# A hybrid decoder layer on one Trainium2 core: the samples' columns join the chunks' columns in the state space products, and the recurrence is spread over more steps

## The chip, the cores and the metric

The kernel runs on one core of a Trainium2 chip. The metric is the device time of one execution in microseconds. An execution uses five engines with queues of their own: TensorE (PE, matrix products, with its weight loads as PEld), VectorE (DVE), ScalarE (ACT), GpSimd (POOL) and SyncE (SP), which issues nearly all transfers. Each engine works through its queue in the order in which the program was written, and waits for others by semaphores.

## The reference

One layer of a hybrid decoder serves one prompt of 2048 tokens and 8 samples of 4 tokens with the same weights, all in fp32. Cut to the part that matters here:

```python
h = rms_norm(x, norm_mix); z = h @ w_in          # [u (512) | xin, B, C (3 x 512)]
y_ssm = s5_ssm(u, ...)                           # 32 groups of 16 channels, one 64-dim complex diagonal state each
#   s[t] = a * s[t-1] + Bbar @ u[t];  y[t] = Re(C @ s[t]) + D * u[t];  samples start from a given state s0
y_ssm = gelu(y_ssm); y_ssm = y_ssm * sigmoid(y_ssm @ w_glu + b_glu)
y_conv = B * causal_dwconv(C * xin, conv_w)      # width 3 over positions
x = x + concat(rms_norm(y_ssm), rms_norm(y_conv)) @ w_out
x = x + cross_attention(...)                     # 4 heads, 256 memory tokens
x = x + (gelu(causal_dwconv(h @ w_up)) * (h @ w_gate)) @ w_down
```

The results are the outputs of prompt and samples, the memory's keys and values, and the new states.

## The kernel before

Columns are positions: the 2048 + 32 tokens lie in five pieces of 416 columns, channels on the partitions. Every weight product is split in three products of rounded fp32 (`mm3`: hi x hi, hi x lo, lo x hi). `W` loads raw weight tiles (`wraw`), rounds them on ScalarE (`whi`) and takes the rest on GpSimd (`wlo`, two halves of 512 columns). `A` does the same for activations: `araw` is scaled and rounded on ScalarE (`xh`), the rest (`xl`) is taken on VectorE for even and on GpSimd for odd tiles. It has ten slots, eight for the piece in work.

The change lies in the second stage, the projections of the short-conv group. It runs over 10 pieces (two halves of five), each with two projections (`ct_`) of three outputs over eight tiles `k`: 20 projections of 72 products, 1440 in all. After each `k`, that is after nine products, a hook runs: in the second projection of a piece it frees the activation tile just used, then weights and activations are pumped, and then the streams `slow` and (every second hook) `slow2` go one step on. I call the nine products a group. After each projection come its convolution products: `xi`, `E` on VectorE, a scaled copy on ScalarE, two taps and a product on VectorE, and the last product `y` on GpSimd, whose store goes out with the next hook.

The state space work is written as generators in the stream `slow`, so a `yield` in them fixes how many groups lie between two of their parts:

- `state_inputs` first runs `phases` up to its mark (the tables of the recurrence, some 70 small VectorE instructions), copies the samples' inputs `us`, and then makes 16 input steps. Step `c` multiplies two input matrices `gc` with the chunk columns `uc` (256 columns, eight tokens each) and, in a second product, with the samples' columns (8), into one PSUM tile; ScalarE copies both into `st`. `turn` (complex turn by `ph`, on VectorE, every third on GpSimd) and `scan_blocks` (a scan of 16 blocks, its factors copied to `dz` by ScalarE) follow one and two steps later.
- `scan` closes the recurrence over the blocks.
- `toeplitz` (in `slow2`) prepares matrices; `state_outputs` waits for it and makes 16 output steps. In step `c`, `enter(c+1)` writes the entry states `scat` and the last state `sfin` (VectorE and GpSimd), `back(c+2)` turns the states back: a product `mc`, a sum, a product `mb` on VectorE, then `st` times `ph` on GpSimd. One group later TensorE multiplies `uc` and `scat` for two channel groups, and with two more products `us` and the samples' entry states `s0s`. ScalarE's GELU reads the PSUM tile, and the results are stored.

All four or eight products of a step stand in one place of TensorE's queue, and the PSUM tiles of these steps (`aux`) have two buffers. `uc`, `gc`/`tcn`, `scat` and `yg` have two buffers each as well. The loads of step `c+2` are written behind the products of step `c`.

Of the kernel before, what the change touches and what calls it, by code (L numbers as in the profile page):

```python
# [11 lines left out]
F32 = mybir.dt.float32  # L12
# [3 lines left out]
ALU = mybir.AluOpType  # L16
# [14 lines left out]
NCH = 256  # L31
# [6 lines left out]
PAUSE, STALL = "pause", "stall"  # L38
# [170 lines left out]
def tile_hymba_step(ctx: ExitStack, tc: tile.TileContext, I: dict, O: list):  # L209
# [25 lines left out]
    u_d = dt("u_d", [512, NB, NCH])  # L235
# [625 lines left out]
    def load_u(c):  # L861

        uc = py.tile([128, 2, NCH], F32, tag="uc", name="uc", bufs=2)
        for i in range(2):
            g = 2 * c + i
            SY.dma_start(out=uc[:, i, :], in_=u_d[16 * g:16 * g + 16].rearrange("p s c -> s p c"))
        return uc
# [65 lines left out]
    def blocks(c):  # L933
        return st[:, :, c, 8:264].rearrange("p r (k j) -> p r k j", j=16)

# [8 lines left out]
    def scan_blocks(c):  # L944

        S.copy(out=dz[:, :, 1:16], in_=rp[:, c, 0:1].unsqueeze(1).to_broadcast([128, 16, 15]))
        for r in range(2):
            x = st[:, r, c, 8:264]
            V.tensor_tensor_scan(out=x, data0=dz.rearrange("p k j -> p (k j)"), data1=x, initial=0.0, op0=ALU.mult, op1=ALU.add)

    def state_inputs():
# [15 lines left out]
        load(1)  # L967
        for step in tb:
            if step == "tables":
                break  # L970
            yield step
        V.tensor_copy(out=us_[64:128, 0], in_=us_[0:64, 1])
        for _ in range(4):
            yield PAUSE
        for c in range(16):
            uc, gc = ld.pop(c)
            for i in range(2):
                ps = aux()
                PE.matmul(ps[:, 8:264], lhsT=gc[:, i, :], rhs=uc[:, i, :], start=True, stop=True)
                PE.matmul(ps[:, 0:8], lhsT=gc[:, i, :], rhs=us_[:, 0, 2 * c + i, :], start=True, stop=True)  # L980
                h = slice(i * 64, (i + 1) * 64)
                S.copy(out=st[h, 0, c, :], in_=ps[0:64, 0:264])
                S.copy(out=st[h, 1, c, :], in_=ps[64:128, 0:264])
            if c + 2 < 16:
                load(c + 2)
            if c > 0:
                turn(c - 1, G if c % 3 == 1 else V)
            if c > 1:
                scan_blocks(c - 2)
            yield PAUSE  # L990
            next(tb, None)
            if c % 4 == 3:
                yield PAUSE
        turn(15, V)
        scan_blocks(14)
        rs_ = []
        for nm in ("state_ssm_re", "state_ssm_im"):
            r = py.tile([128, 128], F32, tag="sr", name="sr", bufs=2)
            SY.dma_start(out=r, in_=I[nm][0].rearrange("b (g a) n -> (b g) (a n)", a=2))
            rs_.append(r)  # L1000
        yield PAUSE
        scan_blocks(15)
        for _ in tb:
            yield PAUSE
        for _ in range(6):
            yield PAUSE
# [33 lines left out]
    def state_outputs():  # L1040
# [24 lines left out]
        def enter(c):  # L1065

            sc = py.tile([128, 2, 256], F32, tag="scat", name="scat", bufs=2)
            V.memset(sc[:, :, 0:1], 0.0)
            m1, m2 = parts.pop(c)
            for a in range(2):  # L1070
                h = slice(a * 64, (a + 1) * 64)
                for r in range(2):
                    (G if r else V).tensor_tensor(out=sc[r * 64:(r + 1) * 64, a, 1:256], in0=m1[h, r, 0:255],
                                                  in1=m2[h, r, 0:255], op=ALU.add if r else ALU.subtract)
            for r in range(2):
                G.tensor_tensor(out=sfin[:, r, c:c + 1], in0=m1[:, r, 255:256], in1=m2[:, r, 255:256],
                                op=ALU.add if r else ALU.subtract)
            ent_[c] = sc
# [15 lines left out]
        for c in range(16):  # L1094
            if c + 1 < 16:
                enter(c + 1)
            if c + 2 < 16:
                back(c + 2)
            yield PAUSE
            uc, tcn, oc = ld.pop(c)  # L1100
# [12 lines left out]
            G.tensor_copy(out=ysm[:, g2, :], in_=yg[:, :, 256:264])  # L1113
            for i in range(2):
# [17 lines left out]
    def scan():  # L1132
# [3 lines left out]
        cmul(sp_, sf[:, 0], sf[:, 1], s0[:, 0], s0[:, 1], a4[:, 0:1, :].to_broadcast(sh), a4[:, 1:2, :].to_broadcast(sh), sh, "scm")  # L1136
        V.tensor_tensor(out=sf, in0=sf, in1=st[:, :, :, 0:8].rearrange("p r g b -> p r b g"), op=ALU.add)
        yield PAUSE
# [5 lines left out]

        last = st[:, :, :, 8:264].rearrange("p r g (k j) -> p r g k j", j=16)[:, :, :, :, 15]
        m2, e = product_tile("b"), product_tile("b")
# [977 lines left out]
```

## Time and profile before

| what | before |
|---|---|
| median of three runs | 3051.72 us (3048.32 to 3055.66) |
| the profiled execution | 3054.09 us |
| its span, first to last instruction | 3052.0 us |
| mean granted clock | 0.98 |
| TensorE, products / weight loads busy | 2904.3 / 2804.3 us (95% / 92%) |
| VectorE, ScalarE, GpSimd busy | 1474.1 / 1109.6 / 1166.6 us |

The times in the rows further down count from the start of the span. A row of the timeline gives start, length, engine, line, operation, the tile written and the tiles read, the shape, and in brackets the idle time of the engine before it and who ended it. Products overlap: one of 128x416 lasts 0.35 us in the records, and the next starts 0.19 us after it. An fp32 product that is not rounded shows as two passes (x2). Behind the wait of a row the name tells who came last.

### The profile page before, as it was taken

The numbers are of one execution on the slowest core, as the hardware profiler recorded it, in microseconds if no ns is written. First come the engines' busy times: TensorE is split into PE (matmuls) and PEld (weight loads), VectorE is DVE, ScalarE is ACT, GpSimd is POOL, SyncE is SP. The second block draws the span as 40 slices with busy tenths as digits, with TensorE's granted clock in tenths as the row PEclk, the third lists the DMA queues.
The fourth block names the chain that finished last, engine by engine and source line by source line (L and its number), as shares of the span: only waits on it lengthen the run. The fifth ranks groups of instructions, "written<-read, shape, count | busy, mean of one in ns | idle before, by whom it ended". The sixth has DMA issues, their size and how long they took to land.

```text
span 3052.0 us, 42118 instructions
## 1 busy us (share of the span) xinstructions
PE 2904.3 (95%) x15728; PEld 2804.3 (92%) x15728; DVE 1474.1 (48%) x2698; ACT 1109.6 (36%) x2152; POOL 1166.6 (38%) x1304
## 2 busy tenths in 40 slices
PE   7868989989999999999999999999999999999998
PEld 6767989879999998999999999998999999989997
DVE  5769675364444344354643333436433433364444
ACT  5334322354445444343422222224222222243333
POOL 3663484354332003343523323233232232245653
PEclk9888989999999999999999999999999999999999
DMA  8553454365343123665532112124312122134331
GB/s 223 149 155 108 135 165 120 88 177 155 113 151 94 51 61 97 203 215 180 181 119 63 56 55 63 56 62 140 99 56 63 49 63 63 56 119 126 112 110 53
DMA packets 387340, 335.95 MB, mean 110 GB/s; under 512 B 81121, under 2 KB 361239, under 8 KB 387103
## 3 DMA queue, kind: packets, MB, share of 16 engines
q1 hardware_dynamic: 364079, 299.30, 33.1%
q10 hardware_dynamic: 23056, 33.96, 3.1%
q8 instruction: 124, 2.03, 0.3%
q14 instruction: 81, 0.66, 0.1%
HBM read 259.98 MB, written 75.29 MB: 110 GB/s over the span
## 4 chain that ended last, share of the span: by engine, by line
PE 57%; DVE 3%; DMA 1%; issue 1%; POOL 1%; ACT 1%; SPq 0%; ACTq 0%; DVEq 0%; POOLq 0%
PE g L368 5%; PE g L369 5%; PE g L367 5%; PE u L368 5%; PE u L367 5%; PE u L369 5%; PE d L367 5%; PE d L369 5%; PE d L368 5%; PE mm L368 3%; PE mm L369 3%; PE mm L367 3%; PE aux L368 1%; DVE t L1173 1%; POOL wlo L98 0%
## 5 line engine op out<-in xcount | busy, mean ns | idle before, releaser
L98 POOL TENSOR_TENSOR wlo<-wraw,whi 128x512 fp32r<-128x512 f32 x489 | 644.0, 1340 | 896.8 <-ACT whi L94 839.0
L367 PE MATMUL mm<-xh,whi 128*128 128x416 f32 x1600 | 584.2, 365 | 5.0 <-ACT whi L94 3.4
L368 PE MATMUL mm<-xl,whi 128*128 128x416 f32 x1600 | 571.9, 357 | 4.5 <-POOL xl L159 4.5
L369 PE MATMUL mm<-xh,wlo 128*128 128x416 f32 x1600 | 568.0, 355 | 3.0 <-POOL wlo L98 2.9
L2013 DVE TENSOR_TENSOR xac<-d,xac 128x416 f32<-128x416 f32 x440 | 258.5, 591 | 252.4 <-PE d L369 249.3
L94 ACT CAST whi<-wraw 128x1024 fp32r<-128x1024 f32 x256 | 267.0, 1046 | 172.5 <-PE d L368 129.5
L367 PE MATMUL d<-acth,whi 128*128 128x416 f32 x880 | 311.4, 354 | 19.1 <-DVE xac L2013 18.1
L367 PEld LDWEIGHTS mm<-xh,whi 128*128 128x128 f32 x1600 | 308.2, 193 | 12.8 <-ACT whi L94 4.0
L369 PEld LDWEIGHTS mm<-xh,wlo 128*128 128x128 f32 x1600 | 307.5, 192 | 8.2 <-POOL wlo L98 5.7
L368 PEld LDWEIGHTS mm<-xl,whi 128*128 128x128 f32 x1600 | 307.8, 192 | 7.6 <-POOL xl L159 5.9
L368 PE MATMUL u<-xl,whi 128*128 128x416 f32 x880 | 311.8, 354 | 1.4 <-POOL xl L159 0.7
L368 PE MATMUL g<-xl,whi 128*128 128x416 f32 x880 | 311.8, 354 | 0.0
L367 PE MATMUL u<-xh,whi 128*128 128x416 f32 x880 | 309.8, 352 | 1.2 <-ACT xh L158 1.1
L367 PE MATMUL g<-xh,whi 128*128 128x416 f32 x880 | 310.6, 353 | 0.0
L369 PE MATMUL d<-acth,wlo 128*128 128x416 f32 x880 | 309.6, 352 | 0.0
L369 PE MATMUL g<-xh,wlo 128*128 128x416 f32 x880 | 309.6, 352 | 0.0
L369 PE MATMUL u<-xh,wlo 128*128 128x416 f32 x880 | 308.5, 351 | 0.0
L368 PE MATMUL d<-actl,whi 128*128 128x416 f32 x880 | 307.9, 350 | 0.2 <-DVE actl L1994 0.2
L1173 DVE SCALAR_TENSOR_TENSOR t<-E,par,t 128x416 f32<-128x416 f32 (+1 forms) x220 | 154.5, 702 | 265.5 <-ACT t L1981 262.6
L159 POOL TENSOR_TENSOR xl<-araw,xh 128x416 fp32r<-128x416 f32 x100 | 114.6, 1148 | 385.5 <-ACT xh L158 357.6
L367 PEld LDWEIGHTS d<-acth,whi 128*128 128x128 f32 x880 | 165.2, 188 | 28.6 <-DVE xac L2013 25.9
L1990 DVE TENSOR_TENSOR t<-t,g 128x416 f32<-128x416 f32 x110 | 64.6, 587 | 260.3 <-PE g L369 260.1
(466 smaller groups left out, 4999.4 us busy)
## 6 DMA issues: line engine op xcount, KB each, us to landing
wraw<-in_w_up_dram SPq DMA_DIRECT2D x66, 512.0 KB
wraw<-in_w_gate_dram SPq DMA_DIRECT2D x66, 512.0 KB
wraw<-in_w_down_dram SPq DMA_DIRECT2D x66, 512.0 KB
araw<-x SPq DMA_DIRECT2D x120, 208.0 KB
xres<-x SPq DMA_DIRECT2D x80, 208.0 KB
x<-xo ACTq DMA_DIRECT2D x80, 208.0 KB
x<-xT ACTq DMA_DIRECT2D x40, 208.0 KB
araw<-oo SPq DMA_DIRECT2D x40, 208.0 KB
```

What stands on the lines that cost most here:

```text
L94: self.nc.scalar.copy(out=hi, in_=r)
L98: eng.tensor_tensor(out=lo[:, s], in0=r[:, s], in1=hi[:, s], op=ALU.subtract)
L159: (eng or nc.vector).tensor_tensor(out=lo[:, 0:n], in0=src, in1=hi[:, 0:n], op=ALU.subtract)
L367: PE.matmul(ps, lhsT=wh, rhs=xh, start=start, stop=False)
L368: PE.matmul(ps, lhsT=wh, rhs=xl, start=False, stop=False)
L369: PE.matmul(ps, lhsT=wl, rhs=xh, start=False, stop=stop)
L1173: V.scalar_tensor_tensor(out=out[:, 0:n], in0=E[:, tap * w:tap * w + n], scalar=c, in1=out[:, 0:n], op0=ALU.mult, op1=ALU.add)
L1990: V.tensor_tensor(out=t, in0=t, in1=ps_[:, 0:NP], op=ALU.mult)
L2013: V.tensor_tensor(out=x, in0=ps[:, 0:NP], in1=x, op=ALU.add)
```

## The change

It has three parts.

1. `uc` and `scat` get 264 columns instead of 256. GpSimd copies the samples' eight columns behind the chunks', in the input steps from `us`, in the output steps `s0s` into `scat` and `us` into `uc`. A step then needs one product where there were two; the samples' columns of `st` move from the front to the back.
2. In `state_inputs` the tables are no longer run ahead of the first step. `recur` is called twice in each input step and does one portion: the next part of the tables until they are ready, then one scan and one turn. Input steps are 2 or 3 groups apart instead of 1 or 2.
3. In the output steps the two channel groups stand apart by one `yield`, and a further `yield` follows the loads: 4 groups from step to step instead of 2.

```diff
-        uc = py.tile([128, 2, NCH], F32, tag="uc", name="uc", bufs=2)
+        uc = py.tile([128, 2, 264], F32, tag="uc", name="uc", bufs=2)
...
-        for step in tb:
-            if step == "tables":
-                break
-            yield step
+        for _ in range(4):
+            yield PAUSE
         V.tensor_copy(out=us_[64:128, 0], in_=us_[0:64, 1])
-        for _ in range(4):
-            yield PAUSE
+        ready, turned, scanned = False, 0, 0
+
+        def recur(upto, n):
+
+            nonlocal ready, turned, scanned
+            if not ready:
+                ready = next(tb) == "tables"
+                return
+            for _ in range(n):
+                if scanned < turned:
+                    scan_blocks(scanned)
+                    scanned += 1
+                if turned < upto:
+                    turn(turned, G if turned % 3 == 1 else V)
+                    turned += 1
+
         for c in range(16):
             uc, gc = ld.pop(c)
+            G.tensor_copy(out=uc[:, :, 256:264], in_=us_[:, 0, 2 * c:2 * c + 2, :])
+            recur(c, 1)
+            yield PAUSE
             for i in range(2):
                 ps = aux()
-                PE.matmul(ps[:, 8:264], lhsT=gc[:, i, :], rhs=uc[:, i, :], start=True, stop=True)
-                PE.matmul(ps[:, 0:8], lhsT=gc[:, i, :], rhs=us_[:, 0, 2 * c + i, :], start=True, stop=True)
+                PE.matmul(ps[:, 0:264], lhsT=gc[:, i, :], rhs=uc[:, i, :], start=True, stop=True)
...
             if c + 2 < 16:
                 load(c + 2)
-            if c > 0:
-                turn(c - 1, G if c % 3 == 1 else V)
-            if c > 1:
-                scan_blocks(c - 2)
-            yield PAUSE
-            next(tb, None)
-            if c % 4 == 3:
+            yield PAUSE
+            recur(c, 1)
+            if c % 2:
                 yield PAUSE
...
-            sc = py.tile([128, 2, 256], F32, tag="scat", name="scat", bufs=2)
+            sc = py.tile([128, 2, 264], F32, tag="scat", name="scat", bufs=2)
+            G.tensor_copy(out=sc[:, :, 256:264], in_=s0s[:, 2 * c:2 * c + 2, :])
...
                 enter(c + 1)
             if c + 2 < 16:
                 back(c + 2)
-            yield PAUSE
             uc, tcn, oc = ld.pop(c)
+            G.tensor_copy(out=uc[:, :, 256:264], in_=us_[:, 1, 2 * c:2 * c + 2, :])
+            yield PAUSE
...
             for i in range(2):
                 ps = aux()
-                for o, rhs in ((slice(0, 256), uc[:, i, :]), (slice(256, 264), us_[:, 1, 2 * c + i, :])):
-                    PE.matmul(ps[:, o], lhsT=tcn[:, i, :], rhs=rhs, start=True, stop=False)
-                    PE.matmul(ps[:, o], lhsT=oc[:, i, :], rhs=sc[:, i, :] if o.start == 0 else s0s[:, 2 * c + i, :],
-                              start=False, stop=True)
+                PE.matmul(ps[:, 0:264], lhsT=tcn[:, i, :], rhs=uc[:, i, :], start=True, stop=False)
+                PE.matmul(ps[:, 0:264], lhsT=oc[:, i, :], rhs=sc[:, i, :], start=False, stop=True)
                 S.activation(out=yg[:, i, :], in_=ps[:, 0:264], func=AF.Gelu_apprx_tanh)
+                if i == 0:
+                    yield PAUSE
             if c + 2 < 16:
                 load(c + 2)
+            yield PAUSE
```

On TensorE the first input step stands after 6 groups of the stage instead of 9, the last after 43 instead of 27. The first output step stands after 75 groups in both, since both wait for `toeplitz`; the last is at 136 instead of 105, of 160 in all. Three places of the built program show how instructions moved. The lines of the changed kernel are some ten higher than those of the kernel before.

GpSimd at the start of the stage, before (`us` is cleared, then weights and an activation are split, `halc` and what follows belong to the first convolution):

```order
L961 MEMSET us 128x512
L98 TENSOR_TENSOR wlo<-wraw,whi 128x512 x2
L159 TENSOR_TENSOR xl<-araw,xh 128x416
L903 MEMSET dz 128x16
L98 TENSOR_TENSOR wlo<-wraw,whi 128x512 x4
L1191 COPY halc<-E 128x2
```

The same place now:

```order
L961 MEMSET us 128x512
L98 TENSOR_TENSOR wlo<-wraw,whi 128x512 x2
L159 TENSOR_TENSOR xl<-araw,xh 128x416
L98 TENSOR_TENSOR wlo<-wraw,whi 128x512 x4
L989 COPY uc<-us 128x2x8
L903 MEMSET dz 128x16
```

The copy of the samples' columns for the first input step is new, and it stands behind all four halves of the weight splits; the first part of the tables, with `dz`, came behind it.

GpSimd at the output step 5, before (`ysm` collects the samples' results, `xl` is an activation's split):

```order
L1113 COPY ysm<-yg 128x16
L159 TENSOR_TENSOR xl<-araw,xh 128x416
L1073 TENSOR_TENSOR scat<-st,mb 64x255 x2
L1076 TENSOR_TENSOR sfin<-st,mb 128x1 x2
L1062 TENSOR_TENSOR st<-st,ph 128x2x256
```

The same step now:

```order
L1123 COPY ysm<-yg 128x16
L159 TENSOR_TENSOR xl<-araw,xh 128x416
L1075 COPY scat<-s0s 128x2x8
L1081 TENSOR_TENSOR scat<-st,mb 64x255 x2
L1084 TENSOR_TENSOR sfin<-st,mb 128x1 x2
L1069 TENSOR_TENSOR st<-st,ph 128x2x256
L1108 COPY uc<-us 128x2x8
```

Two copies came in: the entry states' columns ahead of `scat`, and the inputs' columns at the end, behind the back turn `st`.

TensorE at an output step, before (a projection's last product, then the first channel group of the step):

```order
L369 MATMUL mm<-xh,wlo 128x416
L1107 MATMUL aux<-uc,tcn 128x256
L1108 MATMUL aux<-scat,tcn 128x256
L1107 MATMUL aux<-us,tcn 128x8
L1108 MATMUL aux<-s0s,tcn 128x8
```

And now, where a group of the projection follows the first channel group at once:

```order
L369 MATMUL mm<-xh,wlo 128x416
L1115 MATMUL aux<-uc,tcn 128x264
L1116 MATMUL aux<-scat,tcn 128x264
L367 MATMUL mm<-xh,whi 128x416
L368 MATMUL mm<-xl,whi 128x416
```

The two narrow products are gone, and the product of `uc` now reads what the GpSimd copy wrote.

## Rows read from the trace of the kernel before

**Rows 1.** Page, granted clock in 40 equal slices of the span, in tenths.
```profile
PEclk9888989999999999999999999999999999999999
```

**Rows 2.** Windows: stretch, length, busy us and instructions per engine, granted clock, DMA.
```profile
182.40:380.30 197.90, 164.18 (x809) 155.87 (x809) 155.65 (x313) 78.64 (x169) 90.12 (x93) 0.90 0.46 127
380.30:594.60 214.30, 200.66 (x1029) 191.64 (x1029) 120.41 (x179) 60.37 (x122) 121.85 (x152) 0.94 0.40 123
502.30:589.00 86.70, 86.70 (x461) 85.80 (x460) 28.91 (x54) 25.71 (x47) 24.91 (x29) 1.00 0.25 71
414.00:423.00 9.00, 8.40 (x25) 7.54 (x26) 8.76 (x10) 3.48 (x7) 7.61 (x6) 0.50 0.44 127
```

**Rows 3.** Waits of TensorE, 185 to 560 us: total us, times, longest.
```profile
PE aux L980 <- DVE us L972: 13.1, 1, 13.1
PE aux L979 <- DMA gc<-g_d: 11.6, 5, 4.3
PE aux L1107 <- ACT yg L1110: 8.3, 3, 4.2
```

**Rows 4.** Timeline, TensorE in an input step at full clock: start, length, instruction.
```profile
266.85 0.59 PE L979 MATMUL aux<-uc,gc 128*128 128x256 f32 x2
267.28 0.28 PE L980 MATMUL aux<-us,gc 128*128 128x8 f32 x2
267.42 0.68 PE L979 MATMUL aux<-uc,gc 128*128 128x256 f32 x2
```

**Rows 5.** Timeline, TensorE in an output step at full clock.
```profile
397.96 0.59 PE L1107 MATMUL aux<-uc,tcn 128*128 128x256 f32 x2
...
398.82 0.28 PE L1107 MATMUL aux<-us,tcn 128*128 128x8 f32 x2
...
399.18 0.68 PE L1107 MATMUL aux<-uc,tcn 128*128 128x256 f32 x2
```

**Rows 6.** Timeline, TensorE, ScalarE and GpSimd around the first input step.
```profile
202.74 0.67 PE L979 MATMUL aux<-uc,gc 128*128 128x256 f32 x2 [3.05 <-DMA uc<-u_d]
216.54 0.60 PE L980 MATMUL aux<-us,gc 128*128 128x8 f32 x2 [13.13 <-DVE us L972]
...
208.84 1.04 ACT L94 CAST whi<-wraw 128x1024 fp32r<-128x1024 f32 x1 [11.00 <-DMA wraw<-in_w_in_dram]
...
209.97 2.52 POOL L98 TENSOR_TENSOR wlo<-wraw,whi 128x512 fp32r<-128x512 f32 x2 [6.11 <-ACT whi L94]
```

**Rows 7.** Timeline, GpSimd at the first output step.
```profile
380.18 6.29 POOL L98 TENSOR_TENSOR wlo<-wraw,whi 128x512 fp32r<-128x512 f32 x4
...
390.13 1.26 POOL L1062 TENSOR_TENSOR st<-st,ph 128x512 f32<-128x512 f32 x1
```

**Rows 8.** Timeline, GpSimd and ScalarE in an output step within a piece's second projection.
```profile
455.32 1.28 POOL L159 TENSOR_TENSOR xl<-araw,xh 128x416 fp32r<-128x416 f32 x1
...
459.97 1.64 POOL L1062 TENSOR_TENSOR st<-st,ph 128x512 f32<-128x512 f32 x1 [0.62 <-DVE mb L1061]
461.55 0.20 POOL L1113 COPY ysm<-yg 128x16 f32<-128x16 f32 x1
...
460.05 0.54 ACT L158 CAST xh<-araw 128x416 fp32r<-128x416 f32 x1 [0.92 <-PE mm L369]
```

**Rows 9.** Timeline, a convolution's first product on VectorE and last on GpSimd.
```profile
443.18 0.58 DVE L1241 TENSOR_TENSOR xi<-mm,rs 128x416 f32<-128x416 f32 x1
...
447.46 1.40 POOL L1261 TENSOR_TENSOR y<-y,rs 128x416 f32<-128x416 f32 x1 [2.58 <-DVE y L1260]
```

**Rows 10.** Timeline, TensorE after a wait: an output step, then the next group's products.
```profile
414.60 1.22 PE L1107 MATMUL aux<-uc,tcn 128*128 128x256 f32 x2 [4.16 <-ACT yg L1110]
...
419.74 0.69 PE L367 MATMUL mm<-xh,whi 128*128 128x416 f32 x1
420.23 0.55 PE L368 MATMUL mm<-xl,whi 128*128 128x416 f32 x1
420.58 0.55 PE L369 MATMUL mm<-xh,wlo 128*128 128x416 f32 x1
```

More of the change, by code (lines that the diff above doesn't have):

```diff
@@ L861, in load_u @@
     def load_u(c):
-        uc = py.tile([128, 2, NCH], F32, tag="uc", name="uc", bufs=2)
+        uc = py.tile([128, 2, 264], F32, tag="uc", name="uc", bufs=2)
         for i in range(2):
             g = 2 * c + i
-            SY.dma_start(out=uc[:, i, :], in_=u_d[16 * g:16 * g + 16].rearrange("p s c -> s p c"))
+            SY.dma_start(out=uc[:, i, 0:NCH], in_=u_d[16 * g:16 * g + 16].rearrange("p s c -> s p c"))
         return uc
@@ L933, in blocks @@
     def blocks(c):
-        return st[:, :, c, 8:264].rearrange("p r (k j) -> p r k j", j=16)
+        return st[:, :, c, 0:256].rearrange("p r (k j) -> p r k j", j=16)
     def turn(c, eng):
@@ L947, in scan_blocks @@
         for r in range(2):
-            x = st[:, r, c, 8:264]
+            x = st[:, r, c, 0:256]
             V.tensor_tensor_scan(out=x, data0=dz.rearrange("p k j -> p (k j)"), data1=x, initial=0.0, op0=ALU.mult, op1=ALU.add)
@@ L967, in state_inputs @@
         load(1)
-        for step in tb:
-            if step == "tables":
-                break
-            yield step
-        V.tensor_copy(out=us_[64:128, 0], in_=us_[0:64, 1])
         for _ in range(4):
             yield PAUSE
+        V.tensor_copy(out=us_[64:128, 0], in_=us_[0:64, 1])
+        ready, turned, scanned = False, 0, 0
[11 more added lines that the diff above has]
+                    turned += 1
         for c in range(16):
             uc, gc = ld.pop(c)
+            G.tensor_copy(out=uc[:, :, 256:264], in_=us_[:, 0, 2 * c:2 * c + 2, :])
+            recur(c, 1)
+            yield PAUSE
             for i in range(2):
                 ps = aux()
-                PE.matmul(ps[:, 8:264], lhsT=gc[:, i, :], rhs=uc[:, i, :], start=True, stop=True)
-                PE.matmul(ps[:, 0:8], lhsT=gc[:, i, :], rhs=us_[:, 0, 2 * c + i, :], start=True, stop=True)
+                PE.matmul(ps[:, 0:264], lhsT=gc[:, i, :], rhs=uc[:, i, :], start=True, stop=True)
                 h = slice(i * 64, (i + 1) * 64)
@@ L985, in state_inputs @@
                 load(c + 2)
-            if c > 0:
-                turn(c - 1, G if c % 3 == 1 else V)
-            if c > 1:
-                scan_blocks(c - 2)
             yield PAUSE
-            next(tb, None)
-            if c % 4 == 3:
+            recur(c, 1)
+            if c % 2:
                 yield PAUSE
-        turn(15, V)
-        scan_blocks(14)
         rs_ = []
@@ L1000, in state_inputs @@
             rs_.append(r)
-        yield PAUSE
-        scan_blocks(15)
+        while scanned < 16:
+            recur(16, 1)
+            yield PAUSE
         for _ in tb:
-            yield PAUSE
-        for _ in range(6):
             yield PAUSE
@@ L1098, in state_outputs @@
                 back(c + 2)
+            uc, tcn, oc = ld.pop(c)
+            G.tensor_copy(out=uc[:, :, 256:264], in_=us_[:, 1, 2 * c:2 * c + 2, :])
             yield PAUSE
-            uc, tcn, oc = ld.pop(c)
             sc = ent_.pop(c)
@@ L1136, in scan @@
         cmul(sp_, sf[:, 0], sf[:, 1], s0[:, 0], s0[:, 1], a4[:, 0:1, :].to_broadcast(sh), a4[:, 1:2, :].to_broadcast(sh), sh, "scm")
-        V.tensor_tensor(out=sf, in0=sf, in1=st[:, :, :, 0:8].rearrange("p r g b -> p r b g"), op=ALU.add)
+        V.tensor_tensor(out=sf, in0=sf, in1=st[:, :, :, 256:264].rearrange("p r g b -> p r b g"), op=ALU.add)
         yield PAUSE
@@ L1143, in scan @@
         yield
-        last = st[:, :, :, 8:264].rearrange("p r g (k j) -> p r g k j", j=16)[:, :, :, :, 15]
+        last = st[:, :, :, 0:256].rearrange("p r g (k j) -> p r g k j", j=16)[:, :, :, :, 15]
         m2, e = product_tile("b"), product_tile("b")
```

## Prediction

> **What bounds the kernel now.** I read the page's slices first. TensorE is full nearly everywhere after slice 8; the slices with a granted clock below full speed lie before it [rows 1]. The change touches one stage there, the projections of the short-conv group with the state space work woven in, 182.4 to 594.6 us. It holds 1440 products of 128x416 in 160 groups of nine. In 502.3 to 589.0 us, where nothing else runs, 459 of them take 86.7 us at full clock [rows 2], 0.189 us each: 272 us of the stage's 412. Then I read the waits of TensorE, which name who came last: VectorE's copy of the samples, the loads of gc, ScalarE's GELU [rows 3]. Those three make 33.0 us. Last I read the timeline around each kind of step, for what a step costs at full clock [rows 4, 5] and what the other engines do meanwhile [rows 6 to 9].
>
> TensorE bounds the kernel, so in this stage I count what its queue waits for, and how far the change moves that. Everything after the stage should keep its length.
>
> **Passes removed.** An input step has two pairs of products, each pair 256 and 8 columns wide, each product in two passes. At full clock the wide one takes 0.43 us from start to start and the narrow one 0.14 [rows 4]. There are 32 pairs. Removing the narrow ones gives 4.5 us, and eight more columns in 256 add 32 x 0.43 / 32 = 0.4: **-4.1 us**. In an output step the two wide products take 0.86 us and the two narrow ones 0.36 [rows 5], 32 times: 11.5 - 0.9 = **-10.7 us**. Together -14.8. The Trainium skill ("TensorE: Matmul & The Clock Gate", "Wait — 56ns, not 53.3ns?") puts the floor from start to start at about 25 ns however narrow a product is. By that estimate the 192 narrow passes would be worth 4.8 us and not 16.0. The rows show 0.07 us and more per narrow pass, so I go by the rows.
>
> **The start.** Now the first input step stands after 9 groups, waits 3.05 us for uc and then 13.13 us for VectorE, which must finish the tables before its copy of the samples [rows 6]. In the changed order it stands after 6 groups, and that copy comes ahead of the tables. But the product now also waits for GpSimd's copy into uc, and the order puts that copy behind four wlo subtractions. The last two of them start at 209.97 us, because ScalarE's whi waits for the weights until 208.84 [rows 6]. The weights' loads stand at the same places of SP's queue, so those times should not move. GpSimd is free at 212.5, its copy takes 0.2 to 0.3 (a copy of that size: 0.20 [rows 8]), and TensorE starts at 212.8 in place of 216.54: 3.7 us earlier, but with 27 products (5.1 us) less behind it. **+1.5 us**: the wait is handed from VectorE to GpSimd.
>
> **The other input steps.** From 182.4 to 380.3 us, 197.9 us [rows 2], TensorE has 675 products (127.6) and 16 steps of 1.3 us (two pairs of 0.57, and some 0.1 where the products change), with transposes 149.4. Of the 48.5 us lost 16.2 are the start's two waits, and I put 5 to its low clock and the first groups. That leaves 27, 11.6 of them waits for gc [rows 3]. Tables, turns and scans are the same instructions, handed out over 37 groups in place of 18, so VectorE, 156 us busy of these 198, gets more room. A load has 5 groups to land in place of 2 or 3, so I take the gc waits as gone. New are the waits for GpSimd's copy where it stands behind the convolution's last product on GpSimd. That chain, from xi on VectorE to the end of y, takes 5.7 us [rows 9], about 5.0 after the projection's last product, and TensorE is back for the next step after 2 groups (3.4 us). With VectorE late once by some 5 us, I take a loss of 19 where 27 was; bounds 8 and 27. **-8 us**.
>
> **The output steps, the term that decides.** From 380.3 to 594.6, 214.3 us [rows 2], TensorE has 765 products (144.6) and 16 steps of 2.6 us (two of 1.22, and the same 0.1 to 0.2), with transposes 187: 27 us go to waits and the low clock now. Steps are now 4 groups apart instead of 2, so the waits for GELU and loads should go: **-27 us**. Against that stands one added line. The samples' copy into uc is written behind the next step's entry (scat, sfin) and the back turn after that (st times ph), and one group ahead of the product that reads it. In the GpSimd order it comes right behind st. So TensorE now waits for work of the steps c+1 and c+2. How late is it?
>
> - Steps 1, 4, 5, 8, 9, 12, 13 lie in projections in which each group frees one activation tile; the next one is split at once. The cast on ScalarE waits for that group's products (0.54 us, [rows 8]), and the xl on GpSimd stands ahead of the step in the same hook. From xl's start to st's end it took 6.3 us, 0.62 of it a wait for VectorE and st slowed to 1.64; with st at 1.26 [rows 7] it is 5.2. With cast and hand-overs 1.0 and two small copies 0.4 the samples' columns are there 6.6 to 7.7 us after the group, and TensorE wants them after 1.9. A wait of 4.7 to 5.8; I take 4.7, because VectorE has twice the time per step. 7 x 4.7 = 33.
> - Step 0: in this trace st ended at 391.4 behind four wlo's (6.3 us from 380.2) and an xl [rows 7]; with the copies 391.8, against TensorE's 380.3: 11.5.
> - Step 2: convolution to y 5.0, two pairs of wlo (6.3 as in [rows 7]), the step 4.3 = 15.6, against 6.1 of 3 groups and half a step: 9.5.
> - Steps 6, 10: 5.0 + 4.3 against 6.1: 3.2 each; step 14 without the back turn 1.7. Steps 3, 7, 11, 15 wait for nothing new, since GpSimd gets their time ahead.
>
> Sum **+62 us** in 12 waits. Each leaves the clock low: after a wait of 4.16 us an output step took 5.1 us in place of 2.5 and products came every 0.35 us [rows 10], with a granted clock of 0.50, the 1.2 GHz level, over 414 to 423 us [rows 2]; that is 2.6 and ten times 0.16, 4.2 us lost. Bounds 0 and 4.2 a wait; I take 2.9, nearer the measured end as the waits are as long, for 11 of them: **+32 us**.
>
> **Sum** on the profiled execution (3054.1 us, span 3052.0): -14.8 + 1.5 - 8 - 27 + 62 + 32 = +45.7, so 3099.8. The median of the runs is 2.4 below: **3097 us**.
>
> **Rivals.**
> - *GpSimd keeps ahead* (the other side). If st is done early enough that the copy is no more than one group (1.7 us) behind the hook, nothing new is waited for and the change does what it describes: -14.8 + 1.5 - 8 to -19 - 27, some -54, **2998 us**. For it: GpSimd is busy 0.57 of the output stretch [rows 2]. Against it: xl's cast waits for TensorE itself [rows 8], so GpSimd can't start early there.
> - *Only the weight splits are late.* If the xl gating costs under a group and just steps 0 and 2 wait: 21 + 2 x 2.9 in place of 94: -22, **3030 us**. It decides at a chain of 1.7 us where the row shows over 5.
> - *The clock costs nothing, the waits stay.* +14, **3065 us**. And at the other end waits of 5.8, 4.2 for each clock fall and the inputs unchanged: +75, **3127 us**. These are my forecast's own bounds.
>
> **Chances.** Forecast with its bounds 0.72; GpSimd ahead 0.11; only the splits 0.08; near no change, with waits of half the size, 0.07; beyond 3130 us 0.02. A measurement of this kernel can tell 0.2% (6 us) from no change. Slower by more 0.74, within 0.07, faster by more 0.19. The range reaches from 3040, below the forecast's low bound because VectorE's and GpSimd's queues may run freer than the rows of a crowded stretch say, to 3130; the two rivals below it are the 0.19 left out.
>
> **What would show it.** Of the changed kernel: TensorE's largest wait should be the output product for GpSimd's uc copy, near 62 us in about 12 pieces, the first over 10 us; the input product's first wait should end on GpSimd near 212.8 us; waits for VectorE's us and for gc should be gone; the stage should end near 640 us, with a granted clock of the output stretch below 0.94; behind it all lengths as now. If the list of waits shows no GpSimd copy, or if waits of 4 us leave the clock at full speed, the forecast fails, on the first with 2998 us. If the start resumes well ahead of 212 us, the weights' loads moved and that step is wrong.

## The result, and the profile of the changed kernel

The changed kernel is slower. Its median is 3124.34 us (3119.02 to 3125.38) against 3053.69 us for the kernel before, measured beside it: a ratio of 1.0229, with a 95% interval of 1.0209 to 1.025. The profiled execution took 3123.47 us, its span 3121.3 us: 69.4 us more than the profiled execution before.

The page's row of the granted clock shows where it is lost. The sixth to the eighth of the 40 slices, each 78 us long, are lower than in [rows 1].

```profile
PEclk9888978899999999999999999999999999999999
```

The waits of TensorE in the stage (182 to 680 us) name the cause. The columns are instruction, who came last, total us, times, and the longest. The answer to [rows 3] has one new line on top:

```profile
PE aux L1115 <- POOL uc L1108: 74.5, 15, 11.9
PE aux L994 <- POOL uc L989: 23.0, 9, 10.1
PE aux L994 <- POOL dz L903: 17.1, 1, 17.1
PE aux L1137 <- DVE sf L1147: 8.5, 1, 8.5
```

The waits for the loads of gc, for GELU and for VectorE's us are gone. In their place TensorE waits 15 times for GpSimd's copy into uc in the output steps, and ten times in the input steps (the third line names `dz`, which ended beside the first of those copies). The last line, the samples' last state, was in no wait before.

The next two lines answer to [rows 2]. They are windows from the last product ahead of the first output step to the stage's end, and of four microseconds behind one of these waits (length, busy us of the five engines, granted clock, DMA share and GB/s):

```profile
388.60:665.30 276.70, 202.24 (x902) 186.89 (x901) 116.51 (x179) 61.28 (x124) 131.21 (x184) 0.86 0.31 95
417.00:421.00 4.00, 3.92 (x10) 3.45 (x11) 0.59 (x1) 0.92 (x2) 0.02 (x1) 0.50 0.00 0
```

No engine works a larger share of the time than it did. GpSimd works 0.47 of it where it worked 0.57, and the clock is 0.86 where it was 0.94. GpSimd does not lack time; its work stands in the wrong order. The timeline of GpSimd and TensorE at output step 1 shows it, to be read beside [rows 8] and [rows 10]:

```profile
410.96 1.42 POOL L159 TENSOR_TENSOR xl<-araw,xh 128x416 fp32r<-128x416 f32 x1 [3.08 <-ACT xh L158]
412.32 0.66 POOL L1075 COPY scat<-s0s 128x16 f32<-128x16 f32 x1
413.06 2.20 POOL L1081 TENSOR_TENSOR scat<-st,mb 64x255 f32<-64x255 f32 x2
415.34 0.33 POOL L1084 TENSOR_TENSOR sfin<-st,mb 128x1 f32<-128x1 f32 x2
415.63 1.26 POOL L1069 TENSOR_TENSOR st<-st,ph 128x512 f32<-128x512 f32 x1
416.83 0.19 POOL L1108 COPY uc<-us 128x16 f32<-128x16 f32 x1
...
417.07 1.25 PE L1115 MATMUL aux<-uc,tcn 128*128 128x264 f32 x2 [5.14 <-POOL uc L1108]
418.12 1.09 PE L1116 MATMUL aux<-scat,tcn 128*128 128x264 f32 x2
...
419.69 0.55 PE L369 MATMUL mm<-xh,wlo 128*128 128x416 f32 x1
420.04 0.55 PE L367 MATMUL mm<-xh,whi 128*128 128x416 f32 x1
```

TensorE could have started at 411.93. The copy it needs takes 0.19 us and needs nothing that GpSimd makes here, but it stands at the end of 5.9 us of an activation's split and of work for the steps 2 and 3. Behind the wait the products come every 0.35 us.

To place the time, I split the stage by TensorE's own products: from the first of its 1440 products to the 646th (the inputs, the recurrence and its close), and from there to the last (the outputs). That leaves out what lies ahead of the stage. There the kernels have the same instructions and yet reach the first product between 182.4 us (the kernel before) and 188.8 us (one of the experiments); 3.2 us of the changed kernel's 69.4 come from that. Behind the stage's last product the changed kernel is 1.4 us shorter.

| stage, us from product to product | 1 to 646 | 646 to 1440 | sum |
|---|---|---|---|
| before | 192.3 | 219.7 | 412.0 |
| changed | 197.5 | 282.0 | 479.5 |

The first half is known to some 2 us only: in the four experiments that leave its instructions as they are in the changed kernel (the copy moved ahead, narrow output products, the input half alone, copies on VectorE) it took 199.6 to 200.1 us.

### The profile page after: what moved, and what is told of

Same layout as the page of the kernel before. It is cut to its first block, busy times and chain, and to the rows that moved or that the text cites. A ratio compares the mean times of both kernels' runs of the same rounds, so it can differ in the third digit from the quotient of the medians.

```text
span 3121.3 us, 41741 instructions
## 1 busy us (share of the span) xinstructions
PE 2899.6 (93%) x15536; PEld 2794.6 (90%) x15536; DVE 1461.2 (47%) x2698; ACT 1109.9 (36%) x2152; POOL 1180.9 (38%) x1352
## 4 chain that ended last, share of the span: by engine, by line
PE 55%; DVE 2%; DMA 2%; issue 1%; POOL 1%; ACT 1%; SPq 0%; ACTq 0%; DVEq 0%; POOLq 0%
PE g L368 5%; PE g L369 5%; PE g L367 5%; PE u L368 5%; PE d L367 5%; PE u L367 5%; PE u L369 5%; PE d L369 5%; PE d L368 5%; PE mm L368 3%; PE mm L367 3%; PE mm L369 3%; DMA out_dram<-orow 1%; PE aux L368 1%; POOL wlo L98 1%
## 5 line engine op out<-in xcount | busy, mean ns | idle before, releaser
L367 PE MATMUL mm<-xh,whi 128*128 128x416 f32 x1600 | 596.9, 373 | 3.6 <-ACT whi L94 3.1
```

The costliest lines, as they stand in the source:

```text
L367: PE.matmul(ps, lhsT=wh, rhs=xh, start=start, stop=False)
```

## The experiments

Each ratio is to the kernel before on the same chip. The experiments ran on three chips, so between experiments, and with the changed kernel, ratios and stage lengths are compared rather than medians. Stage lengths are measured as in the table above, each in one profiled execution.

**The copy moved ahead.** In the changed kernel the copy for an output step is written two groups earlier, in the step before (for step 0 one pause earlier):

```diff
+        def cols(c):
+            G.tensor_copy(out=ld[c][0][:, :, 256:264], in_=us_[:, 1, 2 * c:2 * c + 2, :])
...
-        for _ in range(3):
-            yield PAUSE
+        for _ in range(2):
+            yield PAUSE
+        cols(0)
+        yield PAUSE
...
             uc, tcn, oc = ld.pop(c)
-            G.tensor_copy(out=uc[:, :, 256:264], in_=us_[:, 1, 2 * c:2 * c + 2, :])
...
             if c + 2 < 16:
                 load(c + 2)
+            if c + 1 < 16:
+                cols(c + 1)
             yield PAUSE
```

> The changed kernel with one line moved: GpSimd's copy of the samples' columns into uc for output step c+1 is written in step c, ahead of the pause before the results' copy (for step 0: one pause earlier), so three groups ahead of its product and no longer behind the entry and the back turn. Theory (the copy's place behind st makes TensorE wait): the 74.5 us of waits for that copy fall under 10 us, the clock stays up, and the time is 3015 to 3035 us. Rival (GpSimd as a whole is too late and any read of its work waits): TensorE waits as long, now at the product that reads scat, and the time stays over 3090 us.

It took 3042.46 us, a ratio of 0.9948 (0.9933 to 0.9963). One moved copy turns the loss into a small gain. The stage's second half fell from 282.0 to 195.6 us. The waits of TensorE for this copy are 3 instead of 15, and the product that reads scat waits for nothing:

```profile
PE aux L1119 <- POOL uc L1089: 11.9, 3, 6.7
```

The time lies 7 us above the range expected. The 11.9 us of waits that are left, where under 10 were expected, are a part of that; the rest is not placed. GpSimd's rows ahead of the longest of these waits show where the copy stood:

```profile
428.75 2.66 POOL L98 TENSOR_TENSOR wlo<-wraw,whi 128x512 fp32r<-128x512 f32 x2
431.35 0.39 POOL L1089 COPY uc<-us 128x16 f32<-128x16 f32 x1
```

Here it stood behind weight splits. The rival (GpSimd is late whatever it is asked for) is out.

**Narrow output products in the new spacing.** Both copies of the output steps are gone, and the samples' columns are products of their own again:

```diff
-                PE.matmul(ps[:, 0:264], lhsT=tcn[:, i, :], rhs=uc[:, i, :], start=True, stop=False)
-                PE.matmul(ps[:, 0:264], lhsT=oc[:, i, :], rhs=sc[:, i, :], start=False, stop=True)
+                for o, rhs in ((slice(0, 256), uc[:, i, 0:256]), (slice(256, 264), us_[:, 1, 2 * c + i, :])):
+                    PE.matmul(ps[:, o], lhsT=tcn[:, i, :], rhs=rhs, start=True, stop=False)
+                    PE.matmul(ps[:, o], lhsT=oc[:, i, :], rhs=sc[:, i, 0:256] if o.start == 0 else s0s[:, 2 * c + i, :],
+                              start=False, stop=True)
```

> The changed kernel with the output steps' narrow products back: separate products of the samples' eight columns read us and s0s as in the kernel before, and both new copies of the output steps are gone; steps stay four groups apart, their channel groups one group apart. Theory (the waits come from the copy): no wait for GpSimd at these products, output waits for GELU and loads gone too, about 11 us of narrow passes more than with the copy moved early: 3025 to 3046 us. Rival (the new spacing or splitting of the steps costs the time): still over 3090 us.

3040.41 us, 0.9947 (0.9932 to 0.9962), as expected: the spacing of four groups and the split channel groups are no loss. The stage's second half is 199.7 us, with a single wait of 4.3 us for a load of tcn. This kernel also prices the narrow passes. The timelines of TensorE in one channel group at full clock, narrow products first, then the wide ones of the kernel with the copy moved:

```profile
501.12 0.59 PE L1114 MATMUL aux<-uc,tcn 128*128 128x256 f32 x2
501.55 0.59 PE L1115 MATMUL aux<-scat,tcn 128*128 128x256 f32 x2
501.99 0.28 PE L1114 MATMUL aux<-us,tcn 128*128 128x8 f32 x2
502.12 0.37 PE L1115 MATMUL aux<-s0s,tcn 128*128 128x8 f32 x2
502.35 0.44 PE L367 MATMUL mm<-xh,whi 128*128 128x416 f32 x1
502.62 0.34 PE L368 MATMUL mm<-xl,whi 128*128 128x416 f32 x1
```
```profile
536.25 0.61 PE L1119 MATMUL aux<-uc,tcn 128*128 128x264 f32 x2
536.70 0.61 PE L1120 MATMUL aux<-scat,tcn 128*128 128x264 f32 x2
536.95 0.55 PE L367 MATMUL mm<-xh,whi 128*128 128x416 f32 x1
537.34 0.34 PE L368 MATMUL mm<-xl,whi 128*128 128x416 f32 x1
```

From the first product to the projection's second it is 1.50 us with narrow products and 1.09 without: 0.41 us for each of 32 pairs, 13.1 us. (The two kernels are equally fast all the same: the 11.9 us of waits that the early copy had left take up more than half of it.) The Trainium skill ("TensorE: Matmul & The Clock Gate", "Wait — 56ns, not 53.3ns?") puts the least distance from start to start at about 25 ns. By that estimate the four narrow passes of a pair would cost 0.1 us; no product in these rows is that cheap, and the measurement decides.

**The wide products alone.** The kernel before, with the output steps widened and the two copies at the places the change gives them, but still two groups from step to step and the input steps untouched:

```diff
         def enter(c):
...
+            G.tensor_copy(out=sc[:, :, 256:264], in_=s0s[:, 2 * c:2 * c + 2, :])
...
                 back(c + 2)
-            yield PAUSE
             uc, tcn, oc = ld.pop(c)
+            G.tensor_copy(out=uc[:, :, 256:264], in_=us_[:, 1, 2 * c:2 * c + 2, :])
+            yield PAUSE
```

> The kernel before with only the output steps widened: two copies on GpSimd (scat from s0s ahead of the entry, uc from us behind the back turn, one group ahead of the products), two wide products for four; the input steps, the spacing of two groups and the order of the rest are as before. Theory (the copy's place decides, whatever the spacing): waits for that copy of some 4.7 us in most steps and a low clock after them, 3110 to 3150 us. Rival (it needs the wider spacing or the split groups to hurt): 3043 us, the narrow passes saved.

3097.42 us, 1.0129 (1.0114 to 1.0144): 40 us slower than before, below the range expected but on its side, and far from the rival's 3043. The second half of the stage is 261.7 us, and the wait is there in the old spacing too:

```profile
PE aux L1108 <- POOL uc L1101: 58.2, 14, 11.3
```

So the copy in its place is enough to lose time without the wider spacing. The 14 waits here are 4.2 us in the mean, shorter than I had put them.

**The input steps as before.** The changed kernel with `state_inputs` of the kernel before (narrow products, no copies, tables first):

```diff
-            G.tensor_copy(out=uc[:, :, 256:264], in_=us_[:, 0, 2 * c:2 * c + 2, :])
-            recur(c, 1)
-            yield PAUSE
...
+            if c > 0:
+                turn(c - 1, G if c % 3 == 1 else V)
+            if c > 1:
+                scan_blocks(c - 2)
+            yield PAUSE
+            next(tb, None)
```

> The changed kernel with the input steps of the kernel before (tables ahead of the first step, narrow products, spacing of one or two groups, six pauses before the states' transposes); the output steps are the changed ones. From the traces: at the stage's product 1125 the changed kernel is 8.4 us late. Theory (the input half loses, by the start and by a wait of 8.5 us for the samples' last state that comes with the removed pauses): about 3114 us, and that wait is gone. Rival (the input half gains its 10 us and the loss lies elsewhere): 3134 us.

3117.33 us, 1.0194 (1.0177 to 1.0211). Its ratio is below the changed kernel's 1.0229, with intervals that just overlap, and its stage is 6.1 us shorter (473.4), 4.7 of it in the first half. The wait for the last state is gone. The input half loses, as the first theory said.

**The input half alone.** The reverse, with the output steps of the kernel before:

```diff
-                PE.matmul(ps[:, 0:264], lhsT=tcn[:, i, :], rhs=uc[:, i, :], start=True, stop=False)
-                PE.matmul(ps[:, 0:264], lhsT=oc[:, i, :], rhs=sc[:, i, :], start=False, stop=True)
+                for o, rhs in ((slice(0, 256), uc[:, i, 0:256]), (slice(256, 264), us_[:, 1, 2 * c + i, :])):
+                    PE.matmul(ps[:, o], lhsT=tcn[:, i, :], rhs=rhs, start=True, stop=False)
+                    PE.matmul(ps[:, o], lhsT=oc[:, i, :], rhs=sc[:, i, :] if o.start == 0 else s0s[:, 2 * c + i, :],
+                              start=False, stop=True)
...
-                if i == 0:
-                    yield PAUSE
             if c + 2 < 16:
                 load(c + 2)
-            yield PAUSE
```

> The input half of the change alone: input steps, the recurrence handed out and the layout of the samples' columns as changed, the output steps as in the kernel before (narrow products, two groups apart, no copies). Theory (the input half loses some 5 us, as the changed kernel's product 1125 comes 5 to 8 us late): 3058 to 3066 us, with some 40 us of waits for GpSimd and 8.5 for the last state before the output steps. Rival (the forecast: the input half by itself gains 10 us): 3045 us.

3067.63 us, a ratio of 1.0031 (1.002 to 1.0043), 9.6 us slower; the stage is 8.8 us longer (420.8), 7.3 of it in its first half. That is the sign of the first theory, and a little more than its range. The forecast had a gain of 10.6 us here. Three waits of the whole change are there again:

```profile
PE aux L994 <- POOL uc L989: 22.9, 9, 10.1
PE aux L994 <- POOL dz L903: 17.1, 1, 17.1
...
PE aux L1134 <- DVE sf L1144: 8.3, 1, 8.3
```

**The six pauses back.** The change also drops six pauses ahead of the states' transposes. The changed kernel with them:

```diff
+        for _ in range(6):
+            yield PAUSE
         for i, r in enumerate(rs_):
```

> The changed kernel with one edit: the six pauses ahead of the states' transposes, which the change removed, are back. Theory (their removal moved the samples' last state ahead of VectorE's scans and tables): TensorE's wait of 8.5 us for it goes and with it about 2 us of low clock, 3113 us. Rival (the work behind it is only pushed later and the first output step waits as much longer): 3124 us.

3122.15 us, 1.021 (1.0195 to 1.0225); the stage is 478.9 us against 479.5. The rival is the nearer: the theory had 11 us less than the changed kernel. By the ratios alone, 1.021 against 1.0229, the gain would be some 6 us, but their intervals overlap. The wait for the last state falls from 8.5 to 4.1 us, and the first output step waits longer instead:

```profile
PE aux L1117 <- POOL uc L1110: 77.3, 15, 14.9
...
PE aux L1139 <- DVE sf L1149: 4.1, 1, 4.1
```

GpSimd reaches the first output step's copy at 401.00 us here and at 400.45 in the changed kernel. From product 466 to product 646 of the stage TensorE gains 3.5 us with the pauses, and at the first output step it waits 3.0 us longer. (Up to product 466, where the pauses do nothing yet, this trace had lost 1.9 us on the changed kernel's, so by the stage the gain may be 0.6 to 2.5 us.) With the output copies as in the change, that wait of 8.5 us costs little of its own.

**Output copies on VectorE.** The copies leave GpSimd and stand one group earlier still:

```diff
+        def cols(c):
+            V.tensor_copy(out=ld[c][0][:, :, 256:264], in_=us_[:, 1, 2 * c:2 * c + 2, :])
...
         back(0)
+        cols(0)
...
             uc, tcn, oc = ld.pop(c)
-            G.tensor_copy(out=uc[:, :, 256:264], in_=us_[:, 1, 2 * c:2 * c + 2, :])
...
                 if i == 0:
+                    if c + 1 < 16:
+                        cols(c + 1)
                     yield PAUSE
```

> The changed kernel with the output steps' copies into uc on VectorE in place of GpSimd, four groups ahead of their product (written after the first channel group of the step before; for step 0 behind its back turn). With the copy early but on GpSimd three waits were left, 11.9 us, where the copy came behind weight splits. Theory (GpSimd's queue is what makes them): they go with their low clock, about 17 us off 3042, so 3025 us. Rival (VectorE is late as well): output waits of 10 us or more for VectorE's copy, over 3040 us.

3038.16 us, 0.9936 (0.992 to 0.9953). No output product waits for a copy any more, and the second half of the stage is 190.8 us, 4.8 less than with the copy early on GpSimd. The whole time fell by 4 us where 17 were expected: two waits for loads of tcn came up, 8.1 us, and by the profiled executions the stage began 2.8 us later.

**The input steps, three ways.** On this kernel, with the six pauses back: narrow products in the new spacing; wide ones with the copies made one or two groups earlier on GpSimd (the first on VectorE, right behind its copy of the samples); and the same with ScalarE in GpSimd's place.

```diff
-                PE.matmul(ps[:, 0:264], lhsT=gc[:, i, :], rhs=uc[:, i, :], start=True, stop=True)
+                PE.matmul(ps[:, 0:256], lhsT=gc[:, i, :], rhs=uc[:, i, 0:256], start=True, stop=True)
+                PE.matmul(ps[:, 256:264], lhsT=gc[:, i, :], rhs=us_[:, 0, 2 * c + i, :], start=True, stop=True)
```

> As out_copy_dve, and the input steps' products are separate again, 256 and 8 columns, with no copy into uc, in the changed spacing of two or three groups and with the recurrence handed out; also the six pauses ahead of the states' transposes are back. Theory (in the input half it is the copy on GpSimd that costs, not the new spacing): the 22.8 us in 9 waits go, the first step's wait falls from 17.9 to about 9.5 us (samples' inputs were there at 207.0 us), the wait of 8.5 us for the last state goes, some 6 us of narrow passes come back: 2980 to 3000 us. Rival (the new spacing makes TensorE wait for VectorE, ScalarE or loads in these steps): 3010 us or more, with such waits of 15 us or more besides the first.

3026.84 us, 0.9897 (0.9878 to 0.9917): the theory's 2980 to 3000 us is missed, and the time is on the rival's side. In place of the waits for the copies there are 15.1 us of waits for loads of gc, 7.7 of them at the first step. Besides the first step TensorE waits 7.4 us for gc and 2.7 for ScalarE at these products, less than the 15 that the rival named, so the rival's reason is borne out in part.

```diff
+        V.tensor_copy(out=ld[0][0][:, :, 256:264], in_=us_[:, 0, 0:2, :])
...
             yield PAUSE
+            if c + 1 < 16:
+                G.tensor_copy(out=ld[c + 1][0][:, :, 256:264], in_=us_[:, 0, 2 * c + 2:2 * c + 4, :])
             recur(c, 1)
```

> As out_copy_dve, with the input steps wide, but step 0's copy into uc on VectorE right behind its copy of the samples, and the others on GpSimd one or two groups earlier than in the change, ahead of that place's part of the recurrence; six pauses ahead of the states' transposes are back. Theory (place of the copy): the first step starts near 207.5 us in place of 214.9, the other waits fall from 22.8 us to 5 or less, the last state's wait goes: 2980 to 2998 us. Rival (one or two groups are not enough in front of GpSimd's weight splits and last convolution products): waits of 10 us or more remain, about 3005 us.

3030.89 us, 0.9914 (0.9893 to 0.9935). The first step did start at 206.74 us, but 23.7 us of waits for the other copies remained: the rival's reason, though the time is above its 3005 us as well. GpSimd's rows at the longest of them show that two groups do not bring the copy ahead of a convolution's last product:

```profile
248.29 1.34 POOL L1280 TENSOR_TENSOR y<-y,rs 128x416 f32<-128x416 f32 x1 [2.67 <-DVE y L1279]
249.57 0.59 POOL L1002 COPY uc<-us 128x16 f32<-128x16 f32 x1
```

```diff
-                G.tensor_copy(out=ld[c + 1][0][:, :, 256:264], in_=us_[:, 0, 2 * c + 2:2 * c + 4, :])
+                S.copy(out=ld[c + 1][0][:, :, 256:264], in_=us_[:, 0, 2 * c + 2:2 * c + 4, :])
```

> As wide_in_early, with the input steps' copies into uc for steps 1 to 15 on ScalarE in place of GpSimd, at the same places. There TensorE still waited 23.7 us for GpSimd's copies, 9.5 of it where the copy came behind a convolution's last product. Theory (GpSimd's queue makes these waits): they fall to 10 us or less, ScalarE's or loads of gc among them, and the time is about 3015 us. Rival (the loads of uc and gc or the copied tiles are late anyhow, as the 15.1 us of waits for gc with narrow products hint): 15 us or more of such waits and 3025 us or more.

3024.55 us, 0.9887 (0.9869 to 0.9905). The waits of TensorE show each theory half right:

```profile
PE aux L994 <- DMA gc<-g_d: 14.3, 4, 6.3
PE aux L994 <- DVE uc L971: 9.6, 1, 9.6
...
PE aux L994 <- ACT uc L1002: 3.1, 3, 2.3
```

GpSimd's queue did make the waits for the copies (3.1 us are left), but 14.3 us of waits for loads of gc came up, most of them at other steps than the waits that went: the longest, 6.3 us, stands where the kernel with GpSimd's copies waited 0.3 for the copy. The three kernels lie within about 6 us of one another, and their intervals overlap, so which of them is best stays open. Each is about 1% faster than the kernel before, and about 3% faster than the changed one.

## Why the prediction was right, and where its terms were off

The forecast was 3097 us, slower, within 3040 to 3130. The measured time lies in the range, and the mechanism is the one forecast: TensorE waits in the output steps for GpSimd's copy into uc, written behind the back turn of a later step. The first and the third experiment show it from both sides: take the copy out of its place and the loss is gone; bring the wide output products with their copies into the kernel before, without the new spacing, and most of the loss is there. The size was 69 us and not 46.

**Waits of the output steps: right, a little small.** Forecast 62 us in 12 pieces, measured 74.5 in 15. Eleven of the pieces, all of 4.8 us or more, make 70.8 us; the other four are 0.5, 0.5, 0.5 and 2.3. Step 0: 11.5 forecast, 11.9 measured. Step 2: 9.5 and 10.0. The seven steps behind an activation split: 4.7 each forecast, 5.1 to 6.3 measured. I had taken the low end of my own bounds (4.7 to 5.8) "because VectorE has twice the time per step". The chain does not shorten with that: from xl's start to the end of st it took 5.9 us at step 1, where I had counted 5.2 (the rows that I had gave 5.3: 6.29 less 0.62 and 0.38). Steps 6 and 10: 3.2 forecast, 4.8 measured.

**The low clock: right, a little large in the sum.** Forecast 32 us, 2.9 for each of eleven waits. The second half of the stage without its waits is 282.0 - 74.5 = 207.5 us in the changed kernel and 190.8 - 9.1 = 181.7 with the copies on VectorE (9.1 us are all its waits there). The difference, 25.8 us, is what eleven long waits against two cost beside themselves. Of those two only the one of 5.11 us was followed by slow products, so it is ten falls of the clock more, 2.6 us each. The window behind a wait of 5.14 us has the granted clock 0.50, the 1.2 GHz level.

**Old waits and passes of the output steps: right.** Forecast -27 and -10.7. That second half without waits is 181.7 us against 219.7 before, waits included: -38.0. The passes are 13.1 of it by the rows of two experiments.

**The start: right for the wrong time.** GpSimd's copy behind the weight splits was what TensorE waited for, but weights came later than in the trace of before:

```profile
212.20 2.53 POOL L98 TENSOR_TENSOR wlo<-wraw,whi 128x512 fp32r<-128x512 f32 x2 [5.30 <-ACT whi L94]
214.68 0.19 POOL L989 COPY uc<-us 128x16 f32<-128x16 f32 x1
```

TensorE resumed at 214.93 us, not 212.8; in [rows 6] that split began at 209.97. But the whole stage began 3.2 us later, so the term itself is right: resumed 4.7 us earlier after the stage's start, with 27 products (5.1 us) fewer behind it, +0.3 us where +1.5 was forecast (4.77 against 5.10).

**The other input steps: too hopeful.** Forecast -4.1 for passes and -8 for waits. From where TensorE resumed in the first step to the 466th product of the stage (behind the last input step, ahead of the states' transposes) it is 124.1 us before and 123.4 now, with 27 products more: -5.8. A step at full clock that cost 1.31 us costs 0.88 now (0.69 to the projection's next product and 0.38 to the one behind, less a product's own 0.19). So the passes gave 6.9, and waits and clock grew by 1.1 instead of falling by 8. The waits are the ones I had described, in the longest GpSimd's copy behind the convolution's last product. The timeline of VectorE, GpSimd and TensorE:

```profile
246.10 1.26 DVE L949 TENSOR_TENSOR_SCAN st<-dz,st 128x256 f32<-128x256 f32 x2
247.28 0.66 DVE L939 TENSOR_TENSOR mb<-st,ph 128x512 f32<-128x512 f32 x1
...
249.38 0.58 DVE L1251 TENSOR_TENSOR xi<-mm,rs 128x416 f32<-128x416 f32 x1
...
253.66 1.34 POOL L1271 TENSOR_TENSOR y<-y,rs 128x416 f32<-128x416 f32 x1 [2.68 <-DVE y L1270]
254.94 0.59 POOL L989 COPY uc<-us 128x16 f32<-128x16 f32 x1
...
255.59 2.13 PE L994 MATMUL aux<-uc,gc 128*128 128x264 f32 x4 [10.14 <-POOL uc L989]
```

The projection's last product had begun at 240.19 us. VectorE took xi at 249.38, 9 us later, after two scans and two turns of the recurrence and two activation splits that stood ahead of it. From xi to the copy it is the chain that I had counted, 5.6 us. I had let VectorE be late once, by some 5 us, and reckoned that tables, turns and scans over more groups give it room. Instead the same instructions now stand ahead of xi, and what waits for xi has TensorE behind it. This is the step of the prediction that failed; its bound, the input waits unchanged, was the better value.

**The wait I did not have.** The 8.5 us for the samples' last state stand in no term of the prediction; from product 466 to product 646 it is 34.0 us before and 44.6 now, 10.6 more. The change also takes six pauses away ahead of the states' transposes, in a part of the diff that is not printed above, and I had costed their going at nothing. VectorE finishes the last scans and tables, then the last state, and TensorE has come to its transpose before:

```profile
349.89 1.07 DVE L1147 TENSOR_TENSOR sf<-sf,st 128x256 f32<-128x256 f32 x1
...
351.02 0.69 PE L1137 MATMUL aux<-ident,sf 128*128 128x128 f32 x2 [8.53 <-DVE sf L1147]
```

The six pauses alone bring only 0.6 us of stage back in one trace of each kernel, so this counts in the halves of the table and hardly in the whole.

The sum, as measured: +0.3 - 5.8 + 10.6 in the first half, -38.0 + 74.5 + 25.8 in the second, 67.5 us before rounding, against the forecast's 45.7; the stage ended at 665 us and not near 640. Of the difference 16 us lie in the input half and 6 in the output half, where the waits came out 12.5 us above their term and the clock 6 below: part of that agreement is luck. The rival "GpSimd keeps ahead" at 2998 us would have been a gain of 54 us. In the six kernels with the output copies early or gone it was 15 to 34, since the input steps then wait for loads and GpSimd and gain less than forecast.

## What to carry to other kernels

Merging small products into large ones saves passes on TensorE, but it can hand the big product a new condition: a copy of 0.2 us, on another engine's queue, that stands behind work for later steps. When a queue gets a new instruction, write it where its inputs are ready, not where its result is used, and look at what stands ahead of it in that queue; here the same line two groups earlier made the difference between 2% slower and 0.5% faster. When a diff removes pauses, ask for each which engine used that time, even if the wait that comes up is then partly covered by the next one.

## What the runs showed of the hardware

A copy of 128x16 on GpSimd took between 0.19 and 0.66 us. At 416.83 us, with VectorE idle, it took 0.19; at 412.32 us it ran beside a VectorE instruction with two operands in SBUF and took 0.66:

```profile
411.48 1.45 DVE L1067 TENSOR_TENSOR st<-st,mc 128x512 f32<-128x512 f32 x1
412.96 0.69 DVE L1068 TENSOR_TENSOR mb<-st,ph 128x512 f32<-128x512 f32 x1
```

The first of these took 0.69 us with GpSimd idle (376.78 us) and 1.45 here, beside GpSimd's xl. The Trainium skill ("SBUF — State Buffer", "SBUF: two separate sides") says that such instructions of VectorE and GpSimd hold a shared pair of ports one after the other. The rows agree with it. So does the rest of the changed kernel's trace from 150 to 760 us: the 31 copies of this size with VectorE idle took 0.19 to 0.22 us, and the 29 that took 0.39 us or more all ended between 0.01 us ahead of and 0.07 us behind the end of a VectorE instruction beside them. No run took one of the two away, so the cause is not shown by an experiment. In a chain like the one above it adds up: scat took 2.20 us for two instructions at step 1.

In the changed kernel's output steps the clock fell behind the long waits only. Behind the wait of 2.25 us products came every 0.19 us; behind each of the eleven waits of 4.8 us or more the step's first product took 1.04 us to the next, where it takes 0.45 at full clock. The length of the wait alone does not settle it. With the copies on VectorE products came every 0.19 us behind a wait of 3.04 us; in the old spacing with wide products they came every 0.35 us behind one of 2.14 us. The two in this order:

```profile
439.86 0.68 PE L1118 MATMUL aux<-uc,tcn 128*128 128x264 f32 x2 [3.04 <-DMA tcn<-to_d]
...
441.02 0.35 PE L368 MATMUL mm<-xl,whi 128*128 128x416 f32 x1
441.21 0.35 PE L369 MATMUL mm<-xh,wlo 128*128 128x416 f32 x1
```
```profile
450.79 0.71 PE L1108 MATMUL aux<-uc,tcn 128*128 128x264 f32 x2 [2.14 <-POOL uc L1101]
...
454.01 0.55 PE L368 MATMUL mm<-xl,whi 128*128 128x416 f32 x1
454.36 0.55 PE L369 MATMUL mm<-xh,wlo 128*128 128x416 f32 x1
```
